# A decoder step on one core: the opening's three tiles over features are multiplied without the token's factor, and the normalised operands for the other tiles are made beside them in three skewed steps

## The chip, the cores and the metric

The kernel runs on one core of one Trainium2 chip. A core has a matrix engine (TensorE; PE in the profile, and PEld for its weight loads), a vector engine (VectorE, DVE), an activation engine (ScalarE, ACT), a general engine (GpSimd, POOL) and a queue engine (SyncE, SP), each with an instruction queue that is worked off in order, and 16 DMA engines that move data between the chip's main memory and its on-chip memory. Matmuls write into PSUM, a small accumulation memory of eight banks, which DVE and ACT read. The metric is the device time of one execution in microseconds (µs); lower is better.

## What is computed

One layer of a hybrid decoder, for 512 prompt tokens and 64 sample tokens (8 sequences of 8), model width 1024, in single precision. What matters here is its beginning:

```python
cs = silu(c)
mod = cs @ ada_w + ada_b
sh1, sc1, g1, sh2, sc2, g2 = split(mod, 6)
hn = rmsnorm(x, norm1_w) * (1 + sc1) + sh1      # rmsnorm: x * rsqrt(mean(x*x) + eps) * w
u = hn @ w_in
z, xbc, dt_raw, q, k, v, o, ig, fg, xr, gr = split(u)
xbc = silu(causal_conv(xbc, conv_state, conv_w, conv_b))
...
```

`mod` has one row for the prompt and one for each of the eight sample sequences. Behind the input projection come a state-space recurrence (SSD), a matrix memory (mLSTM) and a linear recurrence (RG-LRU), then the output projection, and an MLP of width 4096 with the same kind of modulated norm ahead of it.

Per token, the norm's factor `r = rsqrt(mean(x*x) + eps)` is one number, so

`hn @ w = r * ((x * (1 + sc1) * nw) @ w) + sh1 @ w`.

## The kernel before, in words

**Layout.** Features lie on the partitions: x is eight tiles (k = 0 to 7) of 128 features by 576 tokens. A weight block is 128 output features: eight 128x128 pieces, one for each k. The program is a chain of 125 blocks: block 0 holds the gates, blocks 1 to 44 the input projection (blocks 1, 2 and 3 are the convolution tiles 8, 10 and 0; block 4 is convolution tile 1), then the output projection and the MLP.

**Precision by splitting.** Each operand is split in two, a rounded `hi` (made on ACT) and the rest `lo` (made on DVE), and a product is three matmuls: hi·hi, hi·lo, lo·hi. `mm_k` (L155) issues these for one block and one k, each for both token halves of 288: six matmuls. `w_prep` (L132) splits a weight block: `wh` on ACT (L150), `wl` on DVE (L151).

**The modulation.** `ada_w` is 24 tiles of 1 MB, q = 0 to 23. Tile q below 8 gives shift and scale for features k = q. `ada_mm` (L211) multiplies it with the silu of c and copies the rows out on ACT (L219); `ada_sel` (L222) turns them into columns by a second matmul, and DVE adds the bias into `modt` (L228).

**The opening**, `start` (L327 to L419), runs under `in_order` (L452): every engine's instructions in it keep the order of the program. SP loads the eight x tiles, the first half of the constants `vec`, then ada tiles and weight blocks in turn. ACT and DVE square x, and PE sums the squares over features by narrow matmuls (`sum_tokens`, L265). DVE and POOL make the factor r (`rstd_cols`, L251), and `rstd_bcast` (L272) spreads it over the partitions: transposes on PE, copies on ACT. Dummy matmuls (`warm`, L437) stand between these steps. Then `modulate` (L285), for each k in turn, makes `hn[k]`: scale and factor on DVE (L292) and, for the sample tokens, on POOL (L293 to L295); `hi` on ACT (L297, L298), `lo` on DVE and POOL (L299, L300), and a POOL add (L301) that leaves hn itself in x for the gates. The table TODO says which products of blocks 1, 2 and 3 are issued after which k. They accumulate in three PSUM pairs, `pgs[0..2]`: two from the pool of pairs (which has two), one from single banks. At the end come the gates' matmuls over x (`gates_mm`, L421), their selection by a second matmul (L434), and `ev_gates`.

**After the opening** the scheduler may reorder instructions where data allow it. `unit` (L178) issues one block: 48 matmuls into a PSUM pair, then its eviction. It asks for the weights two blocks ahead (`w_prep(b + 2)`), and twice a unit calls `slot` (L167), which advances every active generator by one step: the gate rows (`gate_rows`, L500), the recurrences, the ada tiles 8 to 23. `conv` (L604) evicts a convolution tile into a row buffer by three ACT copies (L610 to L613), from a pool of four such buffers, and takes four taps: one on ACT, three on DVE (L625). A PSUM pair is free again when its eviction is done; a unit needs a free pair.

**Scheme in the MLP.** `premodulate` and `ev_up` do for the second norm what the change does here for the first: they scale without the factor and apply it at the eviction (DVE, L1272 to L1276; ACT L1277).

Of the kernel before, what the change touches and what calls it, by code (L numbers as in the profile page):

```python
# [22 lines left out]
FT = mybir.dt.float32  # L23
FR = mybir.dt.float32r
# [12 lines left out]
NSH = 10  # L37
# [30 lines left out]
class Kernel:  # L68
# [53 lines left out]
    def w_load(self, upto):  # L122
        while self.w_next_dma <= min(upto, NBLK - 1):
            b = self.w_next_dma
            t = self.T("wg") if b == 0 else self.wpool.tile([128, 1024], FT, name=self.name("raw"), tag="raw", bufs=RAW_BUFS)
            src = self.io["wg"] if b == 0 else self.io["w"][b - 1]
            n = src.shape[1]
            self.nc.sync.dma_start(t[:, :n], src)
            self.w_raw[b] = t[:, :n].rearrange("p (k m) -> p k m", k=8)
            self.w_next_dma += 1  # L130

# [153 lines left out]
    def modulate(self, x, rb, k):  # L285

        nc = self.nc
        amp = self.rpool.tile([128, 9], FT, name=self.name("amp"), tag="amp", bufs=3)
        sc, sh = self.mod("sc1", k), self.mod("sh1", k)
        nc.vector.tensor_scalar(amp, sc, 1.0, self.v("nw1")[:, k:k + 1], op0=OP.add, op1=OP.mult)  # L290
        p, s = x[:, :TP], x[:, TP:].rearrange("p (b t) -> p b t", b=NB)
        nc.vector.scalar_tensor_tensor(p, p, amp[:, 0:1], rb[:, :TP], op0=OP.mult, op1=OP.mult)  # L292
        nc.gpsimd.tensor_tensor(x[:, TP:], x[:, TP:], rb[:, TP:], op=OP.mult)  # L293
        nc.gpsimd.tensor_tensor(s, s, amp[:, 1:, None].to_broadcast([128, NB, 8]), op=OP.mult)
        nc.gpsimd.tensor_tensor(s, s, sh[:, 1:, None].to_broadcast([128, NB, 8]), op=OP.add)  # L295
        hi, lo = self.T("hnh", FR), self.T("hnl", FR)
        nc.scalar.activation(hi[:, :TP], p, AF.Identity, bias=sh[:, 0:1])  # L297
        nc.scalar.activation(hi[:, TP:], x[:, TP:], AF.Copy)  # L298
        nc.vector.scalar_tensor_tensor(lo[:, :TP], p, sh[:, 0:1], hi[:, :TP].bitcast(FT), op0=OP.add, op1=OP.subtract)  # L299
        nc.gpsimd.tensor_tensor(lo[:, TP:], x[:, TP:], hi[:, TP:].bitcast(FT), op=OP.subtract)  # L300
        nc.gpsimd.tensor_scalar(p, p, sh[:, 0:1], None, op0=OP.add)  # L301
        return hi, lo
# [24 lines left out]
    def start(self):  # L327
# [6 lines left out]
        with self.in_order():  # L334
            x = [self.T("x") for _ in range(KT)]
            for k in range(KT):
                nc.sync.dma_start(x[k], io["x"][:, k])
# [10 lines left out]

            def load(q):
                ada[q] = [self.T("ada") for _ in range(4)]  # L350
                for i in range(4):
                    nc.sync.dma_start(ada[q][i][:, :512], io["ada"][q, :, i * 512:(i + 1) * 512])

            for q in range(PAIR_AT):
                load(q)
                self.w_load(W_AT.get(q, 0))
            ms = self.P("ms")
            self.warm(WARM[0])
            for k in range(0, KT, 2):
# [1294 lines left out]
```

## Time and profile before

| | |
|---|---|
| median of 3 runs | 983.16 µs (982.34 to 984.29) |
| the profiled execution | 988.14 µs |
| its span, first to last instruction | 986.4 µs |
| mean granted TensorE clock | 0.983 |
| TensorE busy until 40 µs, windows of 10 | 8.32, 9.78, 9.49, 7.93 |
| VectorE busy in the same windows | 3.88, 2.55, 5.91, 5.38 |
| VectorE busy from 70 to 120, windows of 10 | 7.14, 10.00, 9.15, 9.71, 9.66 |
| weight loads, all 124 blocks | 512.0 KB each |
| ada loads of the opening | 32 of 256.0 KB |

The profiled execution is one among several and here took 988.14 µs, so durations are read from it and the result is compared with the medians. In the profile, a row of the timeline is: start, duration, engine, line, operation, output from inputs, count, and in brackets the time that the engine sat idle before it and whose end released it. A group row gives the count, the busy time, the mean in nanoseconds, and the idle time ahead with its releasers. Matmuls overlap in their pipeline, so the distance between two starts, not the duration of one, is what a matmul costs.

### The profile page before, as it was taken

Reading aid. Unit: us, or ns where it says so; the run is one execution under the profiler, and the core shown is the slowest. Engines: PE = TensorE matmul, PEld = TensorE weight load, DVE = VectorE, ACT = ScalarE, POOL = GpSimd, SP = SyncE. Lnnn points to the kernel's source line nnn. Section 1 sums busy time; section 2 is a strip of 40 time slices with the busy share of each in tenths; the row PEclk is TensorE's granted clock in tenths of the full one; section 3 lists DMA queues with packets and bytes.
Section 4 is the critical chain, followed back from the end, with each engine's and each line's share of the span. In section 5 each row is a group of like instructions: output and inputs, shape, how many; then the busy total and the mean of one; then the engine's idle time right before and its main releaser. Section 6 shows DMA issues by size and latency. Waiting matters only on the chain.

```text
span 986.4 us, 18127 instructions
## 1 busy us (share of the span) xinstructions
PE 962.7 (98%) x7369; PEld 908.2 (92%) x7370; DVE 578.5 (59%) x1206; ACT 400.2 (41%) x741; POOL 140.6 (14%) x194
## 2 busy tenths in 40 slices
PE   9899899999899999999999999999999999999996
PEld 5789888898788899998999999999999999999996
DVE  3659898797866585567444455534553356335544
ACT  3346755554655674535222244312431134114320
POOL 1822212521331222110000000000000000000032
PEclk7999999999899999999999999999999999999998
DMA  9712264765643434434233212222222222222202
GB/s 346 295 66 86 68 180 164 251 206 151 191 160 112 148 108 141 135 124 153 99 110 110 99 66 85 86 87 86 79 72 86 86 86 86 81 77 80 86 22 96
DMA packets 51218, 119.61 MB, mean 121 GB/s; under 512 B 6956, under 2 KB 17468, under 8 KB 51136
## 3 DMA queue, kind: packets, MB, share of 16 engines
q1 hardware_dynamic: 47024, 111.06, 33.3%
q10 hardware_dynamic: 3744, 6.85, 1.8%
q8 instruction: 58, 0.95, 0.4%
q0 software_dynamic: 368, 0.55, 0.2%
q14 instruction: 24, 0.20, 0.1%
HBM read 108.68 MB, written 9.76 MB: 120 GB/s over the span
## 4 chain that ended last, share of the span: by engine, by line
PE 83%; DVE 4%; ACT 3%; DMA 2%; issue 1%; SPq 0%; POOL 0%; POOLq 0%; DVEq 0%; ACTq 0%
PE g L163 72%; PE adap L217 1%; PE g L1379 1%; PE py L734 1%; PE ps L739 1%; DMA cumb<-scr_cum 1%; PE py L737 1%; DMA ada<-ada 1%; PE pu L844 0%; DVE wl L151 0%; PE pn L986 0%; PE lg L1145 0%; DMA nmb<-scr_nm 0%; DVE r L625 0%; PE adas L227 0%
## 5 line engine op out<-in xcount | busy, mean ns | idle before, releaser
L150 ACT ACTIVATE wh<-raw 128x1024 fp32r<-128x1024 f32 x123 | 130.1, 1059 | 348.6 <-PE g L163 326.3
L151 DVE TENSOR_TENSOR wl<-raw,wh 128x1024 fp32r<-128x1024 f32 x123 | 150.7, 1226 | 47.4 <-ACT wh L150 41.9
L163 PE MATMUL g<-hnh,wh 128*128 128x288 f32 x688 | 156.1, 306 | 7.9 <-ACT r L613 5.2
L163 PE MATMUL g<-hnh,wl 128*128 128x288 f32 x688 | 154.8, 304 | 0.5 <-DVE wl L151 0.5
L163 PE MATMUL g<-hnl,wh 128*128 128x288 f32 x688 | 152.7, 300 | 0.0
L163 PEld LDWEIGHTS g<-hnh,wh 128*128 128x128 f32 x688 | 113.0, 192 | 17.6 <-issue 6.5
L163 PEld LDWEIGHTS g<-hnh,wl 128*128 128x128 f32 x688 | 112.9, 191 | 2.4 <-issue 1.1
L163 PEld LDWEIGHTS g<-hnl,wh 128*128 128x128 f32 x688 | 112.8, 191 | 2.0 <-issue 1.6
L163 PE MATMUL g<-h2h,wh 128*128 128x288 f32 (+1 forms) x512 | 111.6, 299 | 0.0
L163 PE MATMUL g<-h2l,wh 128*128 128x288 f32 (+1 forms) x512 | 111.3, 298 | 0.0
L163 PE MATMUL g<-h2h,wl 128*128 128x288 f32 (+1 forms) x512 | 110.8, 298 | 0.0
L163 PE MATMUL g<-hh,wh 128*128 128x288 f32 x480 | 102.7, 295 | 0.0
L163 PE MATMUL g<-hh,wl 128*128 128x288 f32 x480 | 102.5, 294 | 0.0
L306 DVE SCALAR_TENSOR_TENSOR xr<-g,modt,xr 128x288 f32<-128x288 f32 x38 | 19.7, 518 | 141.1 <-PE g L163 141.1
L163 PE MATMUL g<-hl,wh 128*128 128x288 f32 x480 | 102.2, 294 | 0.0
L163 PEld LDWEIGHTS g<-h2l,wh 128*128 128x128 f32 x512 | 84.1, 190 | 0.0
L163 PEld LDWEIGHTS g<-h2h,wh 128*128 128x128 f32 x512 | 83.6, 189 | 0.1
L163 PEld LDWEIGHTS g<-h2h,wl 128*128 128x128 f32 x512 | 83.5, 189 | 0.0
L163 PEld LDWEIGHTS g<-hl,wh 128*128 128x128 f32 x480 | 77.0, 188 | 0.0
L163 PEld LDWEIGHTS g<-hh,wh 128*128 128x128 f32 x480 | 76.8, 188 | 0.0
L163 PEld LDWEIGHTS g<-hh,wl 128*128 128x128 f32 x480 | 76.6, 188 | 0.0
L1421 POOL TENSOR_SCALAR xr<-xr,vec 128x576 f32<-128x576 f32 (+2 forms) x8 | 15.2, 1900 | 385.3 <-ACT sqa L1253 364.5
(398 smaller groups left out, 1534.0 us busy)
## 6 DMA issues: line engine op xcount, KB each, us to landing
raw<-w SPq DMA_DIRECT2D x124, 512.0 KB, 3.5
ada<-ada SPq DMA_DIRECT2D x32, 512.0 KB, 5.0
ada<-ada SPq DMA_DIRECT2D x32, 256.0 KB, 5.8
cumb<-scr_cum SPq DMA_DIRECT2D x16, 256.0 KB, 5.8
s<-s SPq DMA_DIRECT2D x16, 256.0 KB, 4.4
ssm_s<-s ACTq DMA_DIRECT2D x16, 256.0 KB, 4.6
x<-x SPq DMA_DIRECT2D x8, 288.0 KB, 5.0
xr<-x SPq DMA_DIRECT2D x8, 288.0 KB, 3.9
```

The costliest lines, as they stand in the source:

```text
L150: nc.scalar.activation(hi, raw, AF.Copy)
L151: nc.vector.tensor_tensor(lo, raw, hi.bitcast(FT), op=OP.subtract)
L163: self.nc.tensor.matmul(pg.h[h][:m, :e], w(k), xx[:, h * HALF:h * HALF + e], start=start and n == 0, stop=stop and n == 2)
L217: nc.tensor.matmul(ps[32 * j:32 * j + 32, :256], self.cs[:, k, :], ks(k), start=k < 4, stop=k >= 4)
L306: self.nc.vector.scalar_tensor_tensor(dst[:, :HALF], pg.h[0][:, :HALF], gate[:, 0:1], x[:, :HALF], op0=OP.mult, op1=OP.add)
L734: nc.tensor.matmul(o, xdt[:, h * 64:(h + 1) * 64], att[h // 4][:, hs], start=True, stop=not c)
L737: nc.tensor.matmul(o, S[:, h * 64:(h + 1) * 64], ce[h // 4][:, hs], start=False, stop=True)
L739: nc.tensor.matmul(pst, cb[:, 128:256], xend[:, :512], start=True, stop=True)
L1379: nc.tensor.matmul(pgs[i].h[p][:, :c.stop - c.start], w(k), xs[k][x][:, c], start=k == 0 and j == 0, stop=k == 7 and j == 2)
L1421: self.eng("fin").tensor_scalar(x, x, self.v("fnw")[:, o:o + 1], None, op0=OP.mult)
```

## The change

What it does:

- **Operands without the factor.** `scale_only` makes, for each k, `hi` and `lo` of x times (1 + sc1)·w, without r. Ten columns are added behind the tokens; nine hold the shift sh1. Blocks 1, 2 and 3 are multiplied with these operands (`mm` with NSH = 10 extra columns), so that the shift's product stands in the extra columns of the result.
- **The factor at the eviction.** `late_rows` multiplies the PSUM of a block by r and adds the shift's product, into the row buffer of `conv`; `conv` then skips its three ACT copies.
- **The order of the opening** is written out by hand: an ada tile, its selection, a square, products of blocks 1 to 3 for the tiles that are there. The loads follow the list LOADS. The squares are all on ACT, summed on DVE into one tile, and the token sums are taken once.
- **Normalised operands** `hn[k]` for the other blocks are made beside this in three steps, a, b and c, of which c for tile k stands with b of k and a of k + 2. They are made from the scaled columns of `scale_only`. The POOL add into x (L301) goes: x holds hn without the prompt's shift, and one extra column with the shift goes through the gates and is added to their bias in `ev_gates`.
- **Block 4** (convolution tile 1) moves into the opening, in two halves around the gates' matmuls; the gates' selection moves behind its sixth tile.

The core of the diff:

```diff
+    def scale_only(self, x, k):
+        nc = self.nc
+        amp = self.rpool.tile([128, 9], FT, name=self.name("amp1"), tag="amp1", bufs=KT)
+        nc.vector.tensor_scalar(amp, self.mod("sc1", k), 1.0, self.v("nw1")[:, k:k + 1], op0=OP.add, op1=OP.mult)
+        u = self.rpool.tile([128, TS + NSH], FT, name=self.name("xs"), tag="xs", bufs=KT)
+        nc.gpsimd.tensor_copy(u[:, TS:TS + 9], self.mod("sh1", k))
+        nc.gpsimd.memset(u[:, TS + 9:], 0.0)
+        nc.vector.tensor_tensor(u[:, :TS]..., x[:, TP:NT]..., amp[:, 1:, None].to_broadcast([128, NB, 8]), op=OP.mult)
+        n = NT + NSH
+        hi, lo = self.T("hxh", FR, True), self.T("hxl", FR, True)
+        nc.scalar.activation(hi[:, :TP], x[:, :TP], AF.Copy, scale=amp[:, 0:1])
+        nc.scalar.activation(hi[:, TP:n], u, AF.Copy)
+        nc.vector.scalar_tensor_tensor(lo[:, :TP], x[:, :TP], amp[:, 0:1], hi[:, :TP].bitcast(FT),
+                                       op0=OP.mult, op1=OP.subtract)
+        nc.vector.tensor_tensor(lo[:, TP:n], u, hi[:, TP:n].bitcast(FT), op=OP.subtract)
+        return (hi, lo), amp, u
-    def modulate(self, x, rb, k):
...
+    def modulate(self, step, x, k, u, amp):
+        nc = self.nc
+        sh, rb = self.mod("sh1", k), self.rb1
+        p, s = x[:, :TP], x[:, TP:NT]
+        if step == "a":
+            nc.vector.scalar_tensor_tensor(p, p, amp[:, 0:1], rb[:, :TP], op0=OP.mult, op1=OP.mult)
+            nc.gpsimd.tensor_tensor(s, u[:, :TS], rb[:, TP:], op=OP.mult)
+            s3 = s.rearrange("p (b t) -> p b t", b=NB)
+            nc.gpsimd.tensor_tensor(s3, s3, sh[:, 1:, None].to_broadcast([128, NB, 8]), op=OP.add)
+            nc.gpsimd.tensor_copy(x[:, NT:NT + 1], sh[:, 0:1])
+            self.hn[k] = self.T("hnh", FR), self.T("hnl", FR)
+            return
+        hi, lo = self.hn[k]
+        if step == "b":
+            nc.scalar.activation(hi[:, :TP], p, AF.Identity, bias=sh[:, 0:1])
+            nc.scalar.activation(hi[:, TP:], s, AF.Copy)
+        else:
+            nc.vector.scalar_tensor_tensor(lo[:, :TP], p, sh[:, 0:1], hi[:, :TP].bitcast(FT), op0=OP.add, op1=OP.subtract)
+            nc.gpsimd.tensor_tensor(lo[:, TP:], s, hi[:, TP:].bitcast(FT), op=OP.subtract)
+    def late_rows(self, pg):
+        r = self.R()
+        sh = self.rpool.tile([128, 9], FT, name=self.name("shw"), tag="shw", bufs=3)
+        nc.vector.tensor_copy(sh, pg.h[1][:, HALF:HALF + 9])
+        n = TP - HALF
+        s = r[:, 515:603].rearrange("p (b t) -> p b t", b=NB)[:, :, 3:11]
+        nc.vector.tensor_tensor(r[:, 3:3 + HALF], pg.h[0][:, :HALF], self.rb1[:, :HALF], op=OP.mult)
+        nc.vector.tensor_tensor(r[:, 3 + HALF:515], pg.h[1][:, :n], self.rb1[:, HALF:TP], op=OP.mult)
+        nc.vector.tensor_tensor(s, pg.h[1][:, n:HALF]..., self.rb1[:, TP:]..., op=OP.mult)
+        nc.scalar.activation(r[:, 3:515], r[:, 3:515], AF.Identity, bias=sh[:, 0:1])
+        nc.vector.tensor_tensor(s, s, sh[:, 1:, None].to_broadcast([128, NB, 8]), op=OP.add)
+        return r
...
+            ada_mm(0); warm; sel(0); w_prep(1); square(0); square(1); warm; mm(0, 0); ada_mm(1)
+            warm; sel(1); square(2); w_prep(2); warm; mm(0, 1); ada_mm(2); mm(1, 0); sel(2); square(3)
+            mm(1, 1); w_prep(3); mm(0, 2); ada_mm(3); mm(1, 2); square(4); sel(3); square(5)
+            mm(2, 0); mm(2, 1); ada_mm(4); square(6); mm(2, 2); sel(4); square(7); mm(0, 3); mm(1, 3)
+            sum_tokens; r = rstd_cols; mm(2, 3); ada_mm(5); mm(0, 4); sel(5); mm(1, 4)
+            self.rb1 = self.rstd_bcast(r)
+            mm(2, 4)
+            whole(("a", 0), ("a", 1))
+            ada_mm(6); mm(0, 5); sel(6); mm(1, 5)
+            whole(("b", 0), ("c", 0), ("a", 2))
+            mm(2, 5)
+            whole(("b", 1), ("c", 1), ("a", 3))
+            ada_mm(7); mm(0, 6); sel(7); mm(1, 6)
+            whole(("b", 2), ("c", 2), ("a", 4))
+            self.w_prep(4)
+            mm(2, 6)
+            whole(("b", 3), ("c", 3), ("a", 5))
+            for i in range(3): mm(i, 7)
+            whole(("b", 4), ("c", 4), ("a", 6))
+            r0 = self.late_rows(pgs[0])
+            whole(("b", 5), ("c", 5), ("a", 7), ("b", 6), ("c", 6), ("b", 7), ("c", 7))
+            pg = self.PG()
+            for k in range(4):
+                self.mm_k(pg, 4, k, self.hn[k], k == 0, False)
+            ps, g = self.gates_mm(x)
+            r1 = self.late_rows(pgs[1])
+            self.w_load(8)
+            self.w_prep(5)
+            for k in range(4, KT):
+                self.mm_k(pg, 4, k, self.hn[k], False, k == KT - 1)
+                if k == 5:
+                    self.gates_sel(ps, g)
             self.ev_gates(ps)
-            self.ev_conv(pgs[0], 8)
-        self.ev_conv(pgs[1], 10)
-        self.ev_conv(pgs[2], 0)
+        self.ev_conv(pgs[0], 8, r0)
+        self.ev_conv(pgs[1], 10, r1)
+        self.ev_conv(pgs[2], 0, self.late_rows(pgs[2]))
+        self.ev_conv(pg, 1)
...
-WARM = 14, 4, 4, 6
+WARM = 18, 3, 8, 4, 8
+LOADS = [(t[0], int(t[1:] or 0)) for t in "x0 x1 q0 w1 q1 x2 w2 x3 q2 x4 w3 x5 q3 x6 x7 q4 q5 w0 q6 v q7 w4".split()]
```

In the written-out order, calls are put on one line here, `mm(i, k)` is `mm_k` of block 1 + i and tile k, `sel` is `ada_sel` with `scale_only` behind it, and the first half of `vec` is loaded ahead of LOADS. The first unit after the opening is block 5 instead of block 4.

More of the change, by code (lines that the diff above doesn't have):

```diff
@@ L283, in rstd_bcast @@
         return t
-    def modulate(self, x, rb, k):
+    def scale_only(self, x, k):
         nc = self.nc
[L288 to L302, printed above, removed]
@@ L414, in start, with ada_mm, sel @@
-            if not GATES_FIRST:
-                ps = self.gates_mm(x)
+            rows, amps, early, xs = {}, {}, {}, {}
+            sqa = self.T("sqa")[:, :NT]
+            def ada_mm(q):
+                if q < KT:
+                    t = ada.pop(q)
+                    rows[q] = self.ada_mm(lambda k: t[k // 2][:, (k % 2) * 256:(k % 2 + 1) * 256])
+            def sel(q):
+                if q < KT:
+                    self.ada_sel(q, rows.pop(q))
+                    early[q], amps[q], xs[q] = self.scale_only(x[q], q)
@@ new lines, in whole @@
+            def whole(*steps):
+                for step, k in steps:
+                    self.modulate(step, x[k], k, xs[k], amps[k])
+            ada_mm(0)
+            self.warm(WARM[1])
+            sel(0)
+            self.w_prep(1)
+            square(0)
+            square(1)
+            self.warm(WARM[2])
+            mm(0, 0)
+            ada_mm(1)
+            self.warm(WARM[3])
+            sel(1)
+            square(2)
+            self.w_prep(2)
+            self.warm(WARM[4])
+            mm(0, 1)
@@ new lines, in start @@
+            ada_mm(2)
+            mm(1, 0)
+            sel(2)
+            square(3)
+            mm(1, 1)
+            self.w_prep(3)
+            mm(0, 2)
+            ada_mm(3)
+            mm(1, 2)
+            square(4)
+            sel(3)
+            square(5)
+            pgs.append(PairTile(banks=[self.P("g"), self.P("g")]))
+            mm(2, 0)
+            mm(2, 1)
+            ada_mm(4)
+            square(6)
+            mm(2, 2)
+            sel(4)
+            square(7)
+            mm(0, 3)
@@ L635, in conv, with ev_conv @@
         return a, r
-    def ev_conv(self, pg, i):
+    def ev_conv(self, pg, i, rows=None):
         nc = self.nc
@@ L1294, in run @@
         self.start()
-        blk = 4
+        blk = 5
         def inp(evac):
@@ L1300, in inp @@
             blk += 1
-        for i in range(1, 4):
+        for i in range(2, 4):
             inp(lambda pg: self.ev_conv(pg, i))
```

173 lines of the change are left out of this document (83 added, 90 removed).

## The prediction

> **What bounds the kernel now.** Read first the page: the span, then the busy shares.
>
> ```profile
> span 986.4 us, 18127 instructions
> PE 962.7 (98%) x7369; PEld 908.2 (92%) x7370; DVE 578.5 (59%) x1206; ACT 400.2 (41%) x741; POOL 140.6 (14%) x194
> ```
>
> TensorE is busy for 98% of the span, so time can only come out of stretches where it waits, pads or runs at a low clock. The windows by stage show where those are (columns: stage, length, busy µs and instructions of PE, PEld, DVE, ACT, POOL, granted clock, DMA share, GB/s).
>
> ```profile
> 0.00:10.00 10.00, 8.32 (x39) 4.43 (x40) 3.88 (x8) 4.22 (x6) 0.29 (x5) 1.00 0.82 273
> 10.00:20.00 10.00, 9.78 (x51) 6.26 (x51) 2.55 (x13) 2.29 (x6) 1.49 (x2) 0.57 1.04 394
> 20.00:30.00 10.00, 9.49 (x75) 5.12 (x73) 5.91 (x12) 3.33 (x7) 5.70 (x9) 0.75 1.01 373
> 30.00:40.00 10.00, 7.93 (x64) 6.52 (x64) 5.38 (x10) 3.44 (x7) 8.48 (x13) 0.83 1.05 405
> ...
> 60.00:70.00 10.00, 7.78 (x54) 6.38 (x47) 6.27 (x10) 5.32 (x12) 0.62 (x4) 0.83 0.28 99
> ...
> 80.00:90.00 10.00, 10.00 (x78) 10.00 (x77) 10.00 (x15) 6.17 (x13) 1.89 (x6) 1.00 0.28 94
> ```
>
> For 40 µs the DMA engines are full: 2.73, 3.94, 3.73 and 4.05 MB, 14.45 MB in sum. The opening's loads (x, vec, eight ada tiles, five weight blocks) come to 13.7 MB by their shapes, so the last lands at about 38 µs in any order. The weight loads of PE are thin until 40 µs (4.43 to 6.52 of 10), at clocks of 0.57 to 0.83: PE pads. Then the timeline of PE:
>
> ```profile
> 27.57 0.53 PE L163 MATMUL g<-hnh,wh 128*128 128x288 f32 x2
> ...
> 33.92 0.54 PE L163 MATMUL g<-hnh,wh 128*128 128x288 f32 x2 [1.61 <-ACT wh L150]
> ...
> 58.56 0.42 PE L163 MATMUL g<-hnh,wt 128*128 128x288 f32 x2
> 58.92 2.15 PE L428 MATMUL gp<-x,wg 128*32 128x288 f32 x32
> 61.19 1.21 PE L434 MATMUL gp<-gs,vec 128*96 128x288 f32 x4
> 64.49 0.53 PE L163 MATMUL g<-hnh,wh 128*128 128x288 f32 x2 [2.10 <-ACT r L613]
> ...
> 66.32 0.68 PE L163 MATMUL g<-hnh,wh 128*128 128x288 f32 x2
> ...
> 72.47 0.42 PE L163 MATMUL g<-hnh,wh 128*128 128x288 f32 x2
> ```
>
> The three opening blocks 1 to 3 run from 27.57, wait 1.61 µs for a weight split, and end at 58.98, some 20 µs after the last load. Then come the gates, a hole of 2.10 µs in which block 4 waits for the eviction of pgs[0], and a stretch at half clock (pairs of 0.68 for 0.42). Block 4 ends at 72.47, and from there one block follows another. **72.47 is the mark:** the opening's gain is 72.47 less the time at which the same work (blocks 1 to 3, gates, block 4) is done after the change.
>
> **The change, part by part.** Durations first, from PE rows, from the first transpose and the first use of the token factor, and from groups of instructions of the opening.
>
> ```profile
> 41.01 0.43 PE L163 MATMUL g<-hnh,wh 128*128 128x288 f32 x2
> ...
> 41.81 0.51 PE L227 MATMUL adas<-vec,adarow 128*128 128x9 f32 x4
> 42.24 1.07 PE L217 MATMUL adap<-ada,cs 128*32 128x256 f32 x16
> 43.24 0.53 PE L163 MATMUL g<-hnh,wh 128*128 128x288 f32 x2
> ```
> ```profile
> 17.52 1.11 PE L277 MATMUL ba<-vec,col 128*128 128x128 f32 x4
> ...
> 19.46 0.32 POOL L293 TENSOR_TENSOR x<-x,rb 128x64 f32<-128x64 f32 x1 [2.15 <-ACT rb L282]
> ```
> ```profile
> L151 DVE TENSOR_TENSOR wl<-raw,wh 128x1024 fp32r<-128x1024 f32 x5 | 6.4, 1301 | 4.9 <-ACT wh L150 4.9
> L292 DVE SCALAR_TENSOR_TENSOR x<-x,amp,rb 128x512 f32<-128x512 f32 x8 | 6.4, 797 | 0.4
> L299 DVE SCALAR_TENSOR_TENSOR hnl<-x,modt,hnh 128x512 fp32r<-128x512 f32 x8 | 6.2, 780 | 6.4 <-ACT hnh L297 6.4
> L297 ACT ACTIVATE hnh<-x,modt 128x512 fp32r<-128x512 f32 x8 | 5.8, 720 | 10.4 <-DVE x L292 10.4
> L150 ACT ACTIVATE wh<-raw 128x1024 fp32r<-128x1024 f32 x5 | 5.1, 1046 | 2.7 <-PE g L163 2.7
> ...
> L219 ACT ACTIVATE adarow<-adap 128x256 f32<-128x256 f32 x8 | 3.0, 381 | 13.7 <-PE adap L217 13.7
> L290 DVE TENSOR_SCALAR amp<-modt,vec 128x9 f32<-128x9 f32 x8 | 2.4, 297 | 0.7
> L228 DVE TENSOR_TENSOR modt<-adas,vec 128x18 f32<-128x18 f32 x8 | 1.4, 171 | 7.6 <-PE adas L227 7.6
> ```
>
> By starts, six matmuls of a tile and block cost 0.80, an ada_sel 0.43, an ada_mm 1.00.
>
> (1) *Earlier start.* A tile's operand no longer waits for the token factor. Its chain is ada_mm 1.00 (about 2 at half clock), row copy 0.38, ada_sel 0.43, modt 0.17, amp 0.30, hi 0.72, lo 0.78: 3.8 to 4.8. Tile q0 stands behind 0.9 MB instead of 2.7, so by the 273 GB/s of the first window it is in SBUF at about 9. Operands stand at 13 to 14; the block's split queues behind them (1.05 + 1.30), so the first six matmuls end at 16 to 18; now they begin at 27.57. The second and third tile need the chain again, each behind the last one's split: 5 µs each. That puts the end of mm(0, 2), block 1 with tile 2, at 26 to 28. The stretch is latency, not load, and the padding matmuls in it cost nothing, because PE waits for the operand.
>
> (2) *From there PE is full.* 19 of 24 tile-block groups at 0.80 (15.2), five ada_mm (5.0), five ada_sel (2.2), the token sums and the broadcast (about 1.5, an estimate: four transposes took 1.11 at half clock): 23.9. The token sums add a wait. They are issued behind mm(1, 3), and their input needs the last square and the last add, which stand on ACT and DVE behind the operand of tile 4. Counted from 26: PE reaches them after six groups, two ada_mm and two ada_sel, 7.7, at 33.7; sel(4) ends 1.6 before, at 32.1, and modt, amp, hi, square and add (the last two no longer than hi's 0.72 and lo's 0.78) take 3.0 with hi's sample part: 35.1, 1.4 of wait. The three blocks end at 51.3 to 53.3, take 52.3; now 58.98. The 10 extra columns cost 72 times a few ns, nothing that this sum resolves.
>
> (3) *The new wait.* Block 4 takes the PSUM pair of pgs[0], so it waits for late_rows(pgs[0]). That stands on DVE behind a0 to a6, c0 to c4, the split of block 4 and sel(6), sel(7). Behind the waiting matmul on PE are the gates and all later blocks.
>
> ```profile
> L1273 DVE TENSOR_TENSOR r<-g,rb 128x576 f32<-128x576 f32 x32 | 23.9, 748 | 2.7 <-ACT rb L282 2.7
> L1276 DVE TENSOR_TENSOR r<-r,shw 128x64 f32<-128x64 f32 x32 | 7.0, 218 | 0.0
> L1272 DVE COPY shw<-g 128x9 f32<-128x9 f32 x32 | 5.4, 169 | 59.2 <-PE g L163 59.2
> ```
> ```profile
> 142.01 0.68 DVE L716 TENSOR_TENSOR cumb<-cumb,xbc 128x512 f32<-128x512 f32 x1
> 142.61 0.68 DVE L650 SCALAR_TENSOR_TENSOR xbc<-r,r 128x512 f32<-128x512 f32 x1
> ```
>
> The factor is broadcast behind mm(1, 4), nine groups, three ada_mm, three ada_sel, the sums and the wait after 26 to 28, at 40 to 42, and is usable 1.9 later at most (17.52 to 19.46, at half clock): a0 starts at 41.5 to 43.5. DVE's list, back to back (512 elements start every 0.60): twelve steps 7.2, split 1.2, two sel with amp and operand parts 3.2, and late_rows 1.3, whose nearest rows are those of ev_up (0.17 + 0.75 + 0.22 and one more piece): 12.9. At the 0.79 mean of the single rows: 15.2. So it ends between 54.4 and 58.7; I take **56.5**, the middle, since half the steps wait for ACT. PE then idles 4.2, where it now idles 2.10.
>
> (4) *Behind it:* block 4, 48 matmuls 6.4; gates 2.15; their selection 1.21; and a half-clock stretch like the one now after 2.10 of idling (six pairs, 0.26 more each): 1.5. Together 11.3; the mark becomes 67.8, a gain of **4.7**.
>
> The Trainium skill, TensorE: Matmul & The Clock Gate, Part 1 "The HAM clock gate", has the clock halve after at least one idle window of about 3.4 µs. By it a hole under that costs no clock; the trace shows 0.83 for 60 to 70 after 2.10, following 3.4 µs of narrow gate matmuls, and the measurement decides here. By the rule alone the mark would be 1.5 earlier when the hole is short.
>
> (5) *Costed at nothing.* The POOL add into x goes: it hid beside PE, so its end frees POOL, not PE. ACT gets eight more operand copies and eight squares in place of five, some 10 µs, between loads that it waits for anyway (3.33 and 3.44 busy of ten from 20 to 40); DVE's share of the same work counts only where (3) and (6) count it, and would cost up to its whole length if the loads did not cover it. SP issues the same DMAs in another order: vec goes past eight x loads, q0 and q1 past six, and each x still lands before the square that reads it by the bytes ahead of it; block 4's weights stay last of the opening, ahead of the ada tiles of later stages, and block 5 to 8 wait for raw buffers as now. The gates carry one more column; gates_sel moves behind tile 5 of block 4, whose matmuls cover the copies of gs. Were that cover gone, the copies would cost again what now lies between the two gate rows, 0.12 beyond the modelled end of the first. The hole of 2.10 goes: pgs[1]'s eviction, not pgs[0]'s, is next for a PSUM pair, with all of block 4 to hide in.
>
> (6) *Given back later.* DVE enters the next stage with more to do: late_rows twice (2.6) and two splits that are now done before 60 (2.4), 5.0.
>
> ```profile
> 73.51 1.23 DVE L151 TENSOR_TENSOR wl<-raw,wh 128x1024 fp32r<-128x1024 f32 x1 [2.44 <-ACT wh L150]
> ```
> ```profile
> PE g L163 <- ACT r L613: 5.2, 3, 2.1
> ```
>
> DVE now idles for 3.7 of the ten µs from 60 (6.27 busy) and 2.44 ahead of this split, so most of the 5.0 fits. From 80 on it is full (10.00 of 10), and PE already waits 3.1 µs there for evictions (5.2 less the 2.10 above). Bounds: nothing, or all 4.7. I take 1.2, a quarter: the gate rows, a large part of DVE's work there, now also start a unit later.
>
> **Sum.** 4.7 − 1.2 = 3.5. The profiled execution took 988.14 (span 986.4), 5.0 above the median of 983.16; it becomes 984.6, and the median **979.7**.
>
> **Rivals.** *No hole* (0.16): DVE runs back to back and PE never waits for late_rows. Mark 53.3 + 6.4 + 2.15 + 1.21 = 63.1, 9.4 gained, 1.2 given back: 975.0. For it: the 0.60 pace exists. Against: each c needs ACT's b, and each sel on the way waits for PE.
>
> *The hole doubles* (0.26): POOL sets the pace of the skewed steps.
>
> ```profile
> 33.00 0.32 POOL L300 TENSOR_TENSOR hnl<-x,hnh 128x64 fp32r<-128x64 f32 x1 [0.37 <-ACT hnh L298]
> ...
> 37.32 0.74 POOL L300 TENSOR_TENSOR hnl<-x,hnh 128x64 fp32r<-128x64 f32 x1 [0.45 <-ACT hnh L298]
> ```
>
> The same 64-column subtraction takes 0.32 alone and 0.74 when it starts within a DVE step. Each tile has four such POOL operations; with 0.42 on each, a step takes 3.0 on POOL against 1.2 to 1.5 on DVE, and ACT's b waits for it. Three steps lie between sel(7) and late_rows: 4.8 more, mark 72.6, nothing gained, 1.2 given back: 984.3, no change. Against: ACT's waits make DVE pause, and each pause lets POOL in.
>
> The Trainium skill, SBUF — State Buffer, "SBUF: two separate sides", calls the port pair of VectorE and GpSimd an exclusive lock, held for a whole instruction; this speaks against a change that packs two-input DVE steps beside POOL ones. The 0.32 and 0.74 agree with it.
>
> *Slower* (0.12): the chain gates → gate rows → recurrences, not PE, sets the end of the input projections. gate_rows is advanced by slots inside units; block 4 is no unit any more, so the chain starts one unit, 6.3 µs, later against the blocks. If it has no slack before the output projection, 4.7 − 1.2 − 6.3 = −2.8: 986.0. It decides once the slack is under 1.5. Against: PE is full in the window ahead of that end.
>
> ```profile
> 430.00:440.00 10.00, 10.00 (x77) 9.50 (x76) 3.30 (x12) 3.25 (x5) 1.53 (x5) 1.00 0.15 53
> ```
>
>
> *Forecast* (0.46): 977.5 to 981.2.
>
> **Numbers.** A difference of 0.2% (2.0 µs) is about the least that a measurement of this kernel tells from none. Under 981.2: 0.46 + 0.16 = 0.62; within: 0.26; over 985.1: 0.12. The range 974.5 to 985.5 reaches past the first rival and the second; it leaves out about 0.07 below and 0.11 above.
>
> **What would show it.** First block matmul near 15, the three blocks' end near 52, a wait of block 4's first matmul for DVE's late_rows of about 4, the mark near 68. Wrong if a0 starts after 45, if late_rows ends outside 54 to 59, if PE's waits for conv evictions between 75 and 120 grow by more than 2, or if a new PE wait appears between 420 and 460.

## The result and the profile after

The changed kernel takes **1005.63 µs** (median of 4 runs, 1004.35 to 1007.14), the kernel before 982.75 beside it (4 runs, 980.39 to 984.29): a ratio of 1.0228, interval 1.0205 to 1.0251. It is 22.9 µs slower. The forecast was 979.7, faster, with a range of 974.5 to 985.5.

The page of the changed kernel, its span and its busy shares; this execution took 1004.35:

```profile
span 1002.6 us, 18170 instructions
...
PE 965.7 (96%) x7344; PEld 907.1 (90%) x7345; DVE 595.2 (59%) x1248; ACT 407.4 (41%) x755; POOL 128.4 (13%) x202
```

TensorE is busy for nearly the same time (965.7 against 962.7) in a longer span, so most of the time went into waiting. VectorE is busy for 16.7 µs more. The timeline of TensorE, opening to block 6:

```profile
14.25 0.54 PE L165 MATMUL g<-hxh,wh 128*128 128x288 f32 x2 [0.70 <-ACT wh L152]
...
36.56 1.23 PE L271 MATMUL ms<-ones,sqa 128*128 128x1 f32 x10 [1.78 <-DVE col L257]
...
55.04 0.43 PE L165 MATMUL g<-hxh,wt 128*128 128x288 f32 x2
59.86 0.57 PE L165 MATMUL g<-hnh,wh 128*128 128x288 f32 x2 [4.39 <-DVE r L339]
60.23 0.68 PE L165 MATMUL g<-hnl,wh 128*128 128x288 f32 x2
...
64.73 2.15 PE L531 MATMUL gp<-x,wg 128*32 128x288 f32 x32
...
68.50 1.14 PE L541 MATMUL gp<-gs,vec 128*96 128x288 f32 x4
...
82.74 0.85 PE L165 MATMUL g<-hnh,wh 128*128 128x288 f32 x2 [5.14 <-ACT r L726]
83.39 0.68 PE L165 MATMUL g<-hnl,wh 128*128 128x288 f32 x2
```

The early blocks start as foreseen, at 14.25, and end at 55.5; block 4 waits 4.39 for the late rows. The surprise is the last pair of rows: block 6 waits 5.14 for an eviction, and pairs of 0.68 for 0.43 follow, half the clock. The windows from 70 to 90 (columns as in the prediction) show which engine is full meanwhile:

```profile
70.00:80.00 10.00, 7.60 (x58) 7.36 (x56) 9.77 (x18) 5.98 (x10) 0.25 (x2) 1.00 0.46 159
80.00:90.00 10.00, 7.26 (x39) 7.26 (x40) 8.79 (x16) 6.58 (x14) 2.26 (x9) 0.66 0.15 52
```

VectorE, 9.77 of 10; TensorE stands or runs at 0.66 (in the kernel before it is busy for 10.00 of 10 in both windows, at a granted clock of 1.00). And VectorE's own timeline:

```profile
43.27 1.47 DVE L314 SCALAR_TENSOR_TENSOR x<-x,amp,rb 128x512 f32<-128x512 f32 x2
...
61.66 0.81 DVE L314 SCALAR_TENSOR_TENSOR x<-x,amp,rb 128x512 f32<-128x512 f32 x1
...
66.49 0.46 DVE L534 COPY gs<-gp 128x288 f32<-128x288 f32 x1 [2.47 <-PE gp L531]
...
76.00 0.68 DVE L763 SCALAR_TENSOR_TENSOR xbc<-r,r 128x512 f32<-128x512 f32 x1
```

Normalising starts at 43.27 and reaches the eighth tile at 61.66. The gates' matmuls need that tile, and on TensorE they stand behind the half of block 4 that waited for the late rows; they start at 64.73. Behind the gates' copy (66.49) stand the evictions of four blocks, the first of which is done at 76.8. In the kernel before, normalising starts 21 µs earlier:

```profile
22.00 0.87 DVE L292 SCALAR_TENSOR_TENSOR x<-x,amp,rb 128x512 f32<-128x512 f32 x1
```

Further on the waits go on. The largest of TensorE's waits in the changed kernel from 56 to 300 µs:

```profile
PE g L165 <- ACT r L726: 7.8, 2, 5.1
PE g L165 <- DVE r L339: 4.4, 1, 4.4
PE py L847 <- DVE att L824: 3.3, 1, 3.3
PE pin L967 <- ACT cc L953: 1.2, 1, 1.2
```

The best ledger is the start of each block's first matmul, read from the timelines of the profiled executions (e1 to e16 are the experiments below):

| block | before | after | e1 | e4 | e10 | e12 | e13 | e16 |
|---|---|---|---|---|---|---|---|---|
| 4 | 64.5 | 59.9 | 61.6 | 62.2 | 59.5 | 60.9 | 59.8 | 59.6 |
| 5 | 72.5 | 71.1 | 73.3 | 70.2 | 69.6 | 72.5 | 66.3 | 70.8 |
| 7 | 85.2 | 91.3 | 93.7 | 82.9 | 90.3 | 90.3 | 79.0 | 91.3 |
| 14 | 143.3 | 156.8 | 154.5 | 146.7 | 152.7 | 150.5 | 139.6 | 152.4 |
| 24 | 276.7 | 294.6 | 287.2 | 281.1 | 284.1 | 277.3 | 266.0 | 285.4 |
| 45 | 457.8 | 475.4 | 467.8 | 469.9 | 464.6 | 458.0 | 447.2 | 466.0 |

Against the profiled execution of before the change is 1.4 ahead at block 5, 6.1 behind at block 7, 13.5 at block 14 and 17.9 at block 24; from there to block 45 nothing more is lost. Some of the recorded expectations below speak of 13.5 µs lost between blocks 14 and 24. By this table the loss between those two blocks is 4.4, and 7.4 are lost between blocks 7 and 14.

### The profile page after: what moved, and what is told of

Its sections match the earlier page's. It is cut to its first block, busy times and chain, and to the rows that moved or that the text cites. A ratio compares the mean times of both kernels' runs of the same rounds, so it can differ in the third digit from the quotient of the medians.

```text
span 1002.6 us, 18170 instructions
## 1 busy us (share of the span) xinstructions
PE 965.7 (96%) x7344; PEld 907.1 (90%) x7345; DVE 595.2 (59%) x1248; ACT 407.4 (41%) x755; POOL 128.4 (13%) x202
## 4 chain that ended last, share of the span: by engine, by line
PE 86%; DVE 6%; ACT 4%; issue 2%; DMA 1%; POOL 0%; SPq 0%; POOLq 0%; DVEq 0%; ACTq 0%
PE g L165 73%; PE adap L219 2%; DMA ada<-ada 1%; PE g L1492 1%; DVE wl L153 1%; PE py L847 1%; PE ps L852 1%; PE adas L229 1%; PE py L850 1%; PE pn L1099 1%; PE pc L950 0%; PE pu L957 0%; PE pu L1107 0%; DVE att L820 0%; ACT wh L152 0%
## 5 line engine op out<-in xcount | busy, mean ns | idle before, releaser
L165 PE MATMUL g<-hnh,wh 128*128 128x288 f32 x656 | 150.0, 308 | 13.2 <-ACT r L726 7.8
L165 PE MATMUL g<-hnh,wl 128*128 128x288 f32 x656 | 148.4, 305 | 0.0
L165 PE MATMUL g<-hnl,wh 128*128 128x288 f32 x656 | 146.6, 302 | 0.0
L165 PEld LDWEIGHTS g<-hnh,wh 128*128 128x128 f32 x656 | 108.3, 193 | 22.9 <-issue 11.4
L165 PEld LDWEIGHTS g<-hnh,wl 128*128 128x128 f32 x656 | 108.2, 192 | 2.8 <-issue 2.2
L165 PEld LDWEIGHTS g<-hnl,wh 128*128 128x128 f32 x656 | 108.4, 192 | 2.1 <-issue 1.9
```

The costliest lines, as they stand in the source:

```text
L165: self.nc.tensor.matmul(pg.h[h][:m, :e], w(k), xx[:, h * HALF:h * HALF + e], start=start and n == 0, stop=stop and n == 2)
```

## The experiments

Three theories. **S:** block 4 was a unit, and a unit lets the recurrences take two steps; without them the gate rows and all that waits for them come a block later. **V:** VectorE is full behind the opening and paces the evictions. **E:** not its load but the order of the evictions and the four row buffers. Beside them stands **C**, chance: any shift reorders the later work. Each experiment was timed against the kernel before on the same chip; the table gives medians and the ratio with its interval.

| run | µs | before | ratio |
|---|---|---|---|
| e1 two steps back | 999.01 | 982.18 | 1.0140 (1.0088 to 1.0192) |
| e2 block 4's eviction earlier | 1009.79 | 982.18 | 1.0275 (1.0237 to 1.0312) |
| e3 both | 998.75 | 982.18 | 1.0164 (1.0128 to 1.0200) |
| e4 before, two steps out | 998.84 | 982.18 | 1.0167 (1.0119 to 1.0216) |
| e5 e1, fewer taps | 995.34 | 982.40 | 1.0124 (1.0086 to 1.0162) |
| e6 e1, five row buffers | 1000.51 | 982.40 | 1.0178 (1.0141 to 1.0214) |
| e7 before, more for VectorE | 984.44 | 982.40 | 1.0026 (1.0006 to 1.0045) |
| e8 e1, late rows first | 995.37 | 982.40 | 1.0133 (1.0089 to 1.0178) |
| e9 block 4 a unit | 997.89 | 983.84 | 1.0142 (1.0113 to 1.0171) |
| e10 e9, late rows first | 995.60 | 983.84 | 1.0115 (1.0080 to 1.0149) |
| e11 e8, a conv at once | 997.64 | 983.84 | 1.0136 (1.0107 to 1.0165) |
| e12 e1, one tap | 988.81 | 987.71 | 1.0025 (1.0005 to 1.0045) |
| e13 before, one tap | 977.42 | 987.71 | 0.9897 (0.9870 to 0.9924) |
| e14 e10, tap on ACT and POOL | 1003.05 | 987.71 | 1.0144 (1.0112 to 1.0175) |
| e15 before, the same | 994.77 | 987.71 | 1.0073 (1.0044 to 1.0102) |
| e16 e1, no remainders | 993.97 | 982.82 | 1.0104 (1.0054 to 1.0154) |
| e17 e10, split on POOL | 1000.25 | 982.82 | 1.0175 (1.0136 to 1.0214) |
| e18 before, the same | 991.97 | 982.82 | 1.0088 (1.0062 to 1.0115) |

**The lost steps: e1 and e4.**

```diff
         self.ev_conv(pg, 1)
+        self.slot()
+        self.slot()
```

> The changed kernel with the two calls that let the recurrences take a step, which block 4 gave while it was a unit of its own, put back behind the opening's last conv eviction. Theory S (lost steps): the 13.5 us that the changed kernel loses between blocks 14 and 24 come from the recurrences starting one block later; with the steps back that stretch is as before, the 6.4 us lost up to block 7 stay: about 993 us (991 to 996), and the PSUM waits of the attention part between 140 and 290 us fall from 8.7 to about 4.3 us. Theory E (eviction order: block 6 waits for block 4's pair behind three other conv evictions, and what follows is pushed on): nothing of the later stretch depends on the steps, 1004 to 1007 us. Theory C (chance: any shift of the work reshuffles the order and moves the time by some us): anywhere from 985 to 1010, and the stretch from 140 to 290 us is lost or won without the order of PE's work between the blocks being that of the kernel before.

In e4 `unit` skips both calls of `slot` for block 4, in the kernel before:

```diff
-            if i % 4 == 3 and i < len(parts) - 1:
+            if i % 4 == 3 and i < len(parts) - 1 and parts[0][0] != 4:
                 self.slot()
         evac(pg)
-        self.slot()
+        if parts[0][0] != 4:
+            self.slot()
```

> The kernel before, with nothing changed but the two steps that unit 4 lets the recurrences take left out, so that the chain of gate rows starts one block later, as in the changed kernel. Theory S: the same order between the blocks as in the changed kernel and 11 to 14 us lost between blocks 14 and 24: about 995 us (993 to 997). The rival of the prediction that priced this at 6.3 us: 989 us. Theory E: 983 us, as before.

Theory S holds for the stretch that it speaks of. The order of TensorE's instructions is fixed when the program is built, and it can be read there without a run. Matmuls of a block (n:count) and of the recurrences between them, blocks 17 to 20, counted as calls in the program (the traces have the same order, with two instructions for some calls of the recurrences), first the kernel before (e1 has the same counts), then the changed one:

```
17 17:11 pu1 17:4 pu1 17:3 pv4 17:19 pq 17:1 pc4 pu1 17:10 pu1 pin4 pn5 pu6 pi2
18 18:19 pi9 cb2 xt4 18:16 adap8 pj2 pw1 18:2 pw1 18:11 cb2 pj1 xt4 adas2 py8 ps1
19 19:20 cb2 19:4 xt4 19:24
20 20:48 pt4 pt py16 ps1 cb2 xt4 pq4 pk4 adap8 py16 ps1
---
17 17:48 pu2 pin4 pn5 pu6
18 18:20 pi3 18:1 pi8 cb2 18:18 xt4 pc3 pu1 18:6 pc1 18:3 pu1 pin4 adap8 pj2 pw2 cb2 pj1 xt4 pu2 adas2 py8
19 19:18 ps1 19:1 cb2 xt4 19:28 pt2 19:1 pt2 pt py16 ps1
20 20:18 cb2 xt4 20:9 pq4 pk4 20:1 adap8 py16 ps1 20:17 pv4 20:3
```

A block later, the recurrences' matmuls stand closer together, each waiting for the last one's VectorE or ScalarE step, with no block matmuls to fill in. From block 7 to block 24 e1 falls back by 2.0 (from 8.5 to 10.5 behind before), the changed kernel by 11.8. In time the steps are worth 22.9 − 16.8 = **6.1 µs**, half of what was expected; e1's profiled execution is 8.5 behind at block 7 already. e2 and e3 below differ by the same two steps, and there they are worth 1009.79 − 998.75 = 11.0. The longest of e4's TensorE waits from 56 to 300 µs:

```profile
PE py L735 <- DVE att L712: 4.1, 1, 4.1
```

It is the changed kernel's wait for `att` (3.3), in the kernel before. e4 loses 6.7 from block 4 (2.3 ahead of before) to block 24 (4.4 behind), as the rival had it (6.3), and another 7.7 by block 45: between blocks 28 and 30 its order bunches once more, with a 2.0 µs wait for an ada tile. e2 has the same order there and the same loss. The changed kernel lacks the same steps and does not bunch there, so that part goes by C: a reordering that no run here takes apart further.

**The order of the evictions: e2, e3, e6.** e2 swaps the last two lines of the opening, e3 adds the two steps, e6 is e1 with `bufs=5` for the row buffers.

```diff
-        self.ev_conv(pgs[2], 0, self.late_rows(pgs[2]))
         self.ev_conv(pg, 1)
+        self.ev_conv(pgs[2], 0, self.late_rows(pgs[2]))
```

> The changed kernel with block 4's conv eviction put ahead of that of the third early block, so that the PSUM pair which block 6 waits for is read out earlier. Theory E: the wait of 5.14 us at block 6 falls under 1.5 us and the half clock behind it goes, block 7 starts within 1 us of the kernel before, and the gain of about 6 us is kept to the end: about 999.5 us (998 to 1002). Theory S: the same at block 7, and the loss between blocks 14 and 24 stays at 11 to 14 us, so that 999.5 us is its number too. Theory C: the order of the later work changes again, 985 to 1010.

> Both edits of the runs before. If the two losses are separate and add: 1005.6 less 6 less 12, so 987 to 988 us. If the opening's gain of 1.5 us at block 5 then also arrives at the end: 981 to 982 us. Theory E alone: 999 to 1000. Theory C: anywhere from 980 to 1010.

> The changed kernel with the two steps back and five row buffers in place of four, so that block 4's pair can be read out before an earlier convolution has given its buffer back; VectorE has the same to do. Theory E: the wait of 5.1 us at block 6 falls under 2 us and stays away: 993 to 995 us. Theory V: the wait goes from block 6 to one of the blocks behind it, the sum of the waits for evictions between 75 and 130 us stays at 7 to 10 us: 998 to 1000 us.

Theory E falls. Block 6 starts earlier in all three (80.0 against 82.7 after the change; 82.3 and 82.0 against 85.0 in e1), but what it gains is waited for behind it. TensorE's waits, 56 to 300 µs, of e2, and 50 to 140 µs, of e6:

```profile
PE g L165 <- ACT r L726: 7.4, 4, 3.8
```
```profile
PE g L165 <- ACT r L728: 7.0, 2, 4.2
```

In e2 the 7.8 of the changed kernel in two waits became 7.4 in four; e6 has 2.2 less than e1 (9.2) and is no faster. And in e3 the two edits together give what the steps give alone.

**VectorE's load behind the opening: e5, e7, e12, e13.** e5 skips two of three VectorE taps for the three early blocks (the convolution is incomplete), e12 and e13 skip them for all twelve, in e1 and in the kernel before. e7 adds passes that nobody reads:

```diff
             self.ev_gates(ps)
+            d = self.T("dum")
+            for _ in range(6):
+                nc.vector.tensor_tensor(d, rb, rb, op=OP.mult)
             self.ev_conv(pgs[0], 8)
```

> The changed kernel with the two steps back (as in the first experiment, 999.0 us, where block 11 starts 11.8 us later than in the kernel before) and six of VectorE's passes left out: the convolution of the three early blocks adds one tap of three. That takes 6 x 0.82 = 4.9 us from VectorE between 65 and 90 us and nothing from the other engines. Theory V (VectorE is full from about 70 us on, at 9.8 of 10 us, and paces blocks 5 to 13; each us that the change adds to it there comes out at the end): block 11 starts 4 to 6 us earlier, about 994 us (993 to 995.5). Theory E (the four row buffers and the order of ScalarE's evictions hold block 6 up, however much VectorE has to do): 998 to 1000 us.

> The kernel before with six VectorE passes of 128x576 (about 0.75 us each, 4.5 us) put between the gates and the first conv eviction, whose result nobody reads. Theory V: the kernel before has room on VectorE between 60 and 80 us (13.4 of 20 us busy) but none from 80 to 110, so half of it or more comes out: block 11 2 to 5 us later, 985 to 988 us. Theory E: the room takes it, block 11 within 1 us, 982 to 984 us. Theory C (any shift reshuffles): over 990 us or under 980.

> The changed kernel with the two steps back (999.0 us, 16.8 more than the kernel before) and two of VectorE's three passes left out in the convolution of all twelve blocks: about 24 x 0.83 = 20 us off VectorE up to block 13, nothing off the other engines. Theory V: the waits for evictions between 75 and 130 us (9.2 us) fall under 2 us and block 11 starts within 3 us of the next run's; the difference to the next run falls from 16.8 to between -2 and 5 us. Theory E or C: the difference stays over 10 us.

> The kernel before with the same two passes left out of the convolution of all twelve blocks, as the control of the run before. Its own waits for evictions (5.2 us) go: 976 to 980 us by all theories.

4.9 µs off VectorE gave 3.7 (e5 against e1, intervals overlap), 4.5 µs on it cost the kernel before 2.0 (e7, between the ranges of E and V). In e7 its waits for evictions, 50 to 140 µs, grew from 5.2 to 7.9:

```profile
PE g L163 <- ACT r L616: 7.9, 4, 3.1
```

But e12 and e13 set the limit of theory V. With 20 µs off VectorE the difference between the two fell from 16.8 only to 988.81 − 977.42 = **11.4 µs**, where V alone expected at most 5. The ledger tells where it arises: e12 is 1.1 behind e13 at block 4, 6.2 at block 5, 11.3 at block 7, and 10.8 at block 45. So 11.4 arise before block 7, and by the medians 5.4 are left for VectorE's load behind the opening. The ratios of the table give another split, 1.0140 for e1 and 1.0025 less 0.9897 for e12 and e13: 13.8 µs and 12.6, with 1.2 left. So VectorE's share behind the opening can't be told from nothing; the part before block 7 can. TensorE's waits from 50 to 140 µs, e12 first:

```profile
PE g L165 <- DVE r L339: 4.4, 1, 4.4
PE g L165 <- ACT r L728: 3.3, 1, 3.3
```
```profile
PE g L163 <- ACT r L613: 2.1, 1, 2.1
```

Of the 11.3 at block 7, 2.2 are there when the three early blocks end (56.5 against 54.3), and 5.6 are longer waits, for the late rows and for an eviction. Of the rest, some 3.6 are half clock behind these waits (blocks 4 and 6 of e12, pairs of matmuls 0.48 apart in place of 0.27). The gates, e12 first:

```profile
66.20 2.15 PE L533 MATMUL gp<-x,wg 128*32 128x288 f32 x32
```
```profile
54.24 2.15 PE L428 MATMUL gp<-x,wg 128*32 128x288 f32 x32
```

The same 32 matmuls start 12.0 later in e12.

**The opening itself: e8 to e11 and e16.** e8 puts `late_rows(pgs[0])` ahead of a5, b4, c4 and a6; e9 undoes block 4 alone (a unit again, the gates straight behind the three blocks); e10 is both; e11 is e8 with `ev_conv(pgs[0], 8, r0)` ahead of the gates' late rows; e16 is e1 without step c.

```diff
-            whole(("b", 3), ("c", 3), ("a", 5))
+            whole(("b", 3), ("c", 3))
             for i in range(3):
                 mm(i, 7)
-            whole(("b", 4), ("c", 4), ("a", 6))
             r0 = self.late_rows(pgs[0])
+            whole(("a", 5), ("b", 4), ("c", 4), ("a", 6))
```

> The changed kernel with the two steps back, and the late rows of the first early block put ahead of two steps of the modulation on VectorE (a of tile 5 and the remainder and a of tiles 4 and 6), so that block 4's pair comes free some 2.5 us earlier and the wait of 4.39 us at 59.9 falls to 1.5 to 2.5 us. If TensorE's own path counts: block 7 and the end 2 to 3 us earlier, 996 to 997 us. Theory V: block 5 earlier by 2 us, block 11 within 1 us of the first experiment, 998 to 1000 us.

> The changed kernel with one part undone: block 4 is a unit behind the opening again (with its two steps for the recurrences), and the gates follow the three early blocks at once, as in the kernel before. Theory V and S together: VectorE gets the gates' rows some 4 us earlier and the conv evictions with them, the steps are where they were: below the first experiment's 999.0 us by 4 to 9, so 990 to 995 us. If the early blocks themselves cost (theory C, or the extra passes of VectorE alone): 997 to 1000 us. If undoing block 4 gives all back and the opening's lead arrives: 978 to 981 us, the prediction's number.

> The kernel of the run before with, in addition, the first early block's late rows ahead of the two modulation steps (as in the eighth experiment, which gave 3.6 us against the first with intervals that overlap). Theory V: VectorE does the same in another order, so within 2 us of the run before; if TensorE's hole at 59.9 us is what counts, 2 to 3 us less than it.

> The kernel of the eighth experiment (two steps back, late rows first; 995.4 us) with the first early block's conv eviction moved ahead of the gates' late part, so that VectorE works at it while it waited 2.5 us for the gates' matmuls and 1.0 us at 60 us. Nothing is removed from any engine. Theory V: VectorE's queue is 3 to 4 us ahead from there on, the waits for evictions between 75 and 130 us fall from 10.3 to 6 or 7 us: 991 to 993 us. Theory E or C: 994 to 999 us.

> The changed kernel with the two steps back (999.0 us; there the gates start at 67.0, block 5 at 73.3 us) and the third of the three skewed steps left out: the remainders of the normalised operands aren't computed, those of the early operands stand in for them. That takes 8 VectorE passes of 0.78 us (6.2 us) and 8 small GpSimd passes out of 45 to 64 us. If VectorE's load holds up the opening: the wait of 4.4 us at block 4 falls under 2 us, the gates start at 60 to 63 us, block 5 at 66 to 70 us, and the end comes 6 to 10 us earlier: 989 to 993 us. If the opening is held up by something else (loads, the order of the steps, GpSimd's chain): block 5 within 2 us of 73.3, the end 996 to 1000 us.

None brings back more than e16's 5.0 µs against e1. e9 is within the intervals of e1, so block 4's place costs nothing measurable beyond its two steps. e10 is the plainest case. Its three blocks end where e1's do (57.2), the wait at block 4 all but goes, and block 5 starts 3.7 earlier than in e1; 3.4 of that are left at block 7 and 3.2 at block 45. So this wait does count at the end, but block 7 is still 5 µs later than in the kernel before, because of the waits for evictions. TensorE's waits, 50 to 300 µs, of e10:

```profile
PE g L165 <- ACT r L717: 11.2, 3, 6.0
...
PE g L165 <- DVE r L339: 0.7, 1, 0.7
```

In all fourteen profiled versions of the change block 7 starts between 90.0 and 95.8, in eight of them between 90.0 and 91.6. What they share is the late copy of the gates on VectorE, behind which the evictions stand: it is at 64.9 to 71.0 µs in the fourteen, and at 56.0 in e13:

```profile
56.00 0.46 DVE L431 COPY gs<-gp 128x288 f32<-128x288 f32 x1 [0.83 <-PE gp L428]
```

In e9, with the gates straight behind the three blocks, their matmuls wait for the normalising steps; TensorE's waits from 50 to 140 µs of it:

```profile
PE gp L522 <- DVE x L314: 3.6, 2, 3.2
```

In e16, VectorE had 6.2 µs less to do in the opening, and the wait at block 4 fell from 4.4 to 2.1. This is what VectorE did with the rest:

```profile
59.58 0.74 DVE L314 SCALAR_TENSOR_TENSOR x<-x,amp,rb 128x512 f32<-128x512 f32 x1
66.19 0.46 DVE L536 COPY gs<-gp 128x288 f32<-128x288 f32 x1 [5.87 <-PE gp L533]
```

It waited 5.87 for the gates' matmuls, which stand behind half of block 4 on TensorE. Blocks 4 to 7 came 2.1 to 2.6 earlier than in e1, between what the two theories expected. e11, which puts an eviction ahead of the gates' late part, makes block 7 later (95.8): TensorE then waits 3.7 for ScalarE's weight split. So the late rows, the late gates and the evictions behind them hold the opening up. That this comes in part from VectorE's load and in part from the order written out by hand fits e8, e10 and e16. But their intervals overlap with e1's, and no run has both e16's lighter VectorE and e10's order, with the gates ahead of block 4, so the two parts are not shown one by one. A version that has both the early blocks and the evictions in time was not found.

**Moving the load: e14, e15, e17, e18.** `CONV = "adda"` in e14 and e15; in e17 and e18 GpSimd makes the weight remainders:

```diff
-                nc.vector.tensor_tensor(lo, raw, hi.bitcast(FT), op=OP.subtract)
+                (nc.gpsimd if 6 <= b < 15 else nc.vector).tensor_tensor(lo, raw, hi.bitcast(FT), op=OP.subtract)
```

> The version of the tenth experiment (block 4 a unit, late rows first; 995.6 us) with the last tap of every convolution made by ScalarE (product) and GpSimd (sum) in place of VectorE: 12 x 0.83 = 10 us off VectorE up to block 13, and the result the same. Theory V: 3 to 8 us gained, 988 to 993 us, less if GpSimd's pass (1.3 to 1.7 us) stands in the way of the tanh behind it. Theory E or C: 994 to 998 us.

> The kernel before with the same last tap on ScalarE and GpSimd, as control. Theory V: VectorE has some room here, so 0 to 3 us gained: 979 to 983 us, if the longer chain of one eviction costs nothing.

> The version of the tenth experiment (995.6 us) with the weight remainders of blocks 6 to 14 made by GpSimd in place of VectorE: 9 x 1.23 = 11 us off VectorE between 70 and 130 us, to an engine that has 80% of its time free and two blocks of lead. If VectorE's load is the cause up to block 13: 3 to 6 us gained, 989 to 993 us. If GpSimd is too slow for it or gets in VectorE's way: 996 to 1005 us.

> The kernel before with the weight remainders of blocks 6 to 14 made by GpSimd in place of VectorE. The eleventh and thirteenth runs say that VectorE is what its evictions wait for (5.2 us in all, 5 to 10 us gained with 20 us off): 977 to 981 us, which would be under both kernels. If GpSimd gets in VectorE's way: 984 to 992 us.

All four medians got worse: e15 and e18 against the kernel before, clear of noise; e14 and e17 against e10, with intervals that overlap. In e15 the GpSimd pass is a link in each eviction's chain; the group of it, 60 to 160 µs:

```profile
L633 POOL TENSOR_TENSOR r<-r,r 128x600 f32<-128x600 f32 x11 | 21.6, 1966 | 13.3 <-DVE r L625 11.1 <-ACT r L630 2.2
```

1.97 µs in place of VectorE's 0.83, longer than the 1.3 to 1.7 expected: VectorE had less to do (53.9 against 59.3 µs busy from 60 to 130), and TensorE's waits for evictions from 50 to 300 µs grew from 5.2 to 8.9 all the same. No version here that computes the whole layer beats the kernel before.

## Why the prediction was wrong

**The base of the sum.** The prediction took the profiled execution, 5.0 above the median, and carried those 5.0 over unchanged. Most of them lay in the part that the change replaces. Five other executions have the same opening (the kernel before with edits behind it: e4, e7, e13, e15, e18); their gates start at 56.63, 52.56, 54.24, 55.56 and 52.39, against 58.92. The windows of e13 from 10 to 30 µs tell why:

```profile
10.00:20.00 10.00, 9.78 (x64) 5.93 (x64) 3.77 (x16) 2.29 (x6) 2.00 (x4) 0.83 1.05 402
20.00:30.00 10.00, 7.68 (x89) 4.99 (x88) 6.49 (x11) 4.92 (x11) 7.80 (x12) 1.00 1.01 353
```

0.83 and 1.00, where the prediction's rows have 0.57 and 0.75: the prediction's execution ran its opening at half clock for longer. After the change the three blocks end at 55.5 in the profiled execution, 3.5 ahead of the quoted row. But eight executions have that opening up to there (the changed kernel, e1, e2, e3, e5, e6, e9, e12): they end the three blocks at 55.5 to 59.3, 57.1 in the mean, and the five others of the kernel before at 54.3 in the mean. So the first matmul stands 10 µs earlier, and the three blocks end 2.7 later (2.0 with the prediction's own execution counted in). The gain of the opening wasn't there against the median.

**Steps 1 and 2** were right in kind: 14.25 for the first matmul, 26.6 for the end of mm(0, 2), a wait of 1.78 for the predicted 1.4. From there to the end of the three blocks it took 28.9, not 25.3. The mis-sized term is the 0.80 for a tile's six matmuls: with the other operations and the waits as measured, 18.0 µs remain for the 19 groups, 0.95 each (one between two ada operations took 0.91, from 39.71 to 40.62).

**Step 3** was right in mechanism, and the late rows ended at 59.7, outside the 54 to 59 named as the bound. That the wait has the predicted size (4.39 for 4.2) is in part luck: the blocks' end and the late rows both came 3.2 late. a0 at 43.27 was as worked out.

**Step 4:** the mark came at 71.1, not 67.8: the gain was 1.4, not 4.7.

**Step 5 failed**, where it says that the hole at the eviction goes, "pgs[1]'s eviction, not pgs[0]'s, is next for a PSUM pair, with all of block 4 to hide in". True of block 5. But block 6 takes block 4's own pair, and its eviction stands behind three others, which stand behind the gates, which stand behind eight tiles that VectorE normalises from 43 µs on in place of 22. The prediction gave that queue no price. In the changed kernel it cost a wait of 5.14 and the half clock behind it, and by e12 and e13 the whole opening costs 11.4 before block 7.

**Step 6 was mis-sized.** "Most of the 5.0 fits", bounds nothing or 4.7. VectorE is busy 16.7 more in the whole span; by e12 and e13 between 1.2 µs of the end (from the ratios) and 5.4 (from the medians) come from its load behind the opening, so the 1.2 that was taken stays possible.

**The rival "Slower"** had the mechanism that the runs confirm, at a price of the right order (6.3; e1 gives 6.1, e2 and e3 11.0, e4 6.7 up to block 24 and 16.7 at the end), and was given 0.12 with the argument that TensorE is full ahead of the projections' end. It is full there because the loss comes earlier, between blocks 7 and 24, in part as waits inside the recurrences. "The hole doubles" did not happen (4.39), "no hole" neither.

Put together, against the medians: 11.4 before block 7, 5.4 through VectorE up to block 13, 6.1 through the lost steps, 22.9. By the ratios of the table the three are 12.6, 1.2 and 8.6. The terms come from differences with intervals of some 5 µs, and they add up because of the way they were formed. The first and the third are clear of noise, the second is not.

## What to carry to other kernels

When a stage is made to start earlier, follow the slowest consumer of what it used to make on the way: here the normalised operands, which the gates need and behind which the evictions stand in order, came late, and the gates with them 12 µs later, so that the first block could begin 10 µs earlier (e12 against e13: 13.8 and 24.0); and not even the three blocks themselves ended earlier. Before a gain is read off a profiled execution that is slower than the median, find where in it the excess lies; if it lies in the part to be changed, it isn't there to be gained. And count the scheduling steps that a piece of code gives to others as part of its work when it is moved.

## What the runs showed of the hardware

**The clock in the opening is not the same from one execution to the next.** The same instructions of the same opening, six matmuls of dummy operands 128x512, took 2.72 µs in the profiled execution of before and 1.46 in e7 (granted clock from 10 to 20 µs 0.57 and 1.00):

```profile
21.26 2.72 PE L441 MATMUL warm<-wz 128*128 128x512 bf16 x6
```
```profile
17.15 1.46 PE L444 MATMUL warm<-wz 128*128 128x512 bf16 x6
```

The Trainium skill, TensorE: Matmul & The Clock Gate, Part 1 "The HAM clock gate", calls the window free-running and the count of cold matmuls variable from run to run, and holds the whole for under 1% of a span; here the gates start up to 6.5 µs of 986 apart (58.92 against 52.39), which agrees.

The same is seen behind a stop. Ahead of block 4 TensorE waits 2.1 µs in all six executions with the opening of before. Behind it block 4 takes 8.0 µs, with a stretch at half clock, in three of them (before, e4, e15), and 6.4 to 6.5 without one in the other three (e7, e13, e18). So the 1.5 that the prediction gave to that stretch is not in every execution.

**VectorE stands until GpSimd's instruction is over.** In e18, GpSimd's weight remainder first, VectorE's rows beside it second:

```profile
87.77 3.36 POOL L151 TENSOR_TENSOR wl<-raw,wh 128x1024 fp32r<-128x1024 f32 x1
```
```profile
87.30 0.45 DVE L493 SCALAR_TENSOR_TENSOR sp_e<-sp_e,sp_z 128x288 f32<-128x288 f32 x1
...
88.91 2.54 DVE L493 SCALAR_TENSOR_TENSOR sp_e<-sp_e,sp_z 128x288 f32<-128x288 f32 x1
```

A pass that takes 0.45 took 2.54 when it began while GpSimd was at work, and ended 0.3 behind GpSimd's instruction. That fits the exclusive lock of the Trainium skill, SBUF — State Buffer, "SBUF: two separate sides", which the prediction weighed in the small (0.32 and 0.74). From 60 to 140 µs VectorE's taps of 128x600 take 1.03 in the mean in e18, against 0.84 in the kernel before; what that alone costs at the end was not measured.
